# A mixture-of-experts layer with two streams of tokens: where the context's column-tiled down products stand in an expert's order of work

## The chip, the cores and the metric

The kernel runs on one core of one Trainium2 chip. The metric is the time of one execution on the device in microseconds; below it is the median of three executions. TensorE (PE) multiplies, VectorE (DVE) and ScalarE (ACT) work elementwise, GpSimd (POOL) here issues gathers and scatters, and SyncE (SP) issues the large loads.

## The reference

Two transformer layers are computed on 1024 latent tokens and 256 context tokens of width 1024. Each layer has attention of two kinds and a convolution, and then a mixture of 16 experts in which each expert picks its own tokens. Only the first layer sends the context through its experts too. What matters here is this part:

```python
def ec_moe(h, w_router, w_gate, w_up, w_down):
    bsz, n_tok, d = h.shape
    cap = EC_CAPACITY * n_tok // N_EXPERTS
    aff = jax.nn.softmax(jnp.einsum('bnd,de->bne', h, w_router).astype(jnp.float32), axis=-1)
    g, idx = lax.top_k(jnp.swapaxes(aff, 1, 2), cap)
    xs = jax.vmap(lambda hb, ib: hb[ib])(h, idx)
    hid = jax.nn.silu(jnp.einsum('becd,edf->becf', xs, w_gate)) * jnp.einsum('becd,edf->becf', xs, w_up)
    ye = jnp.einsum('becf,efd->becd', hid, w_down) * g[..., None].astype(h.dtype)
    return jax.vmap(lambda yb, ib: jnp.zeros((n_tok, d), h.dtype).at[ib.reshape(-1)].add(yb.reshape(-1, d)))(ye, idx)
```

An expert takes 128 latent tokens and 32 context tokens. Everything is float32.

## The kernel before, in words

**Steps and chunks.** The experts of the first layer run in `moe` (from line 2072) as 16 x 12 steps, numbered `i`; step `c` of expert `e` works on one chunk of that expert's weights, 128 x 2048 values, 1 MB. Chunks 0 to 7 are gate and up weights (a gate step: `mm_gu0`, lines 2145 and 2146), chunks 8 to 11 are down weights (a down step).

**Precision.** A chunk is split into a high part (`w_hi`, a copy on ACT to the faster 32-bit matmul type, line 2065) and a low part, the rest (`w_lo`, a subtraction on DVE, line 2071). The latent rows' down product `mm_d0` (lines 2226 to 2228) has for each of 4 pieces of a chunk three matmuls of 128 x 512: high hidden values with the high part, low hidden values with the high part, high hidden values with the low part. So the first two of each three read `hi` alone, and the third reads `lo`.

**The context's down product.** For 32 tokens a full product would fill a quarter of the array. `mm_dc` (line 2217) therefore puts four products side by side, each 32 columns wide, and sums their parts later (`ev_dc`). It reads the raw chunk, without any split, in full float32, which takes two passes a matmul: 8 passes a chunk in the trace. In the loop it stands ahead of `mm_d0` in each of the four down steps. For the last expert the down steps are written out behind the loop, and there the four chunks' `mm_dc` stand in a row ahead of all of `mm_d0`.

**Order.** The order on every engine is the order in which the program issues the instructions. A step issues its matmuls; then the evacuations of the step before (`ev_gu`, `ev_d`, `ev_dc`); then the high part of the chunk three steps ahead and the low part of the chunk two steps ahead (`self.w_hi(i + m - 1)`, `self.w_lo(l, i + m - 2, nc.vector)`, with four pairs of slots, m = 4); then the loads; then transposes of the next expert's gathered tokens (`xprep`, at c = 7 the latent rows, at c = 9 the context rows, line 2129). Besides, every seventh step loads 1 MB of the next layer's modulation weights (`adw`), and DVE reduces it in pairs of operations (`adj`, line 366) four and five steps later.

**Loads.** Raw chunks go round seven buffers (four `raw`, three `more`). All of them, and `adw`, are issued by SP in order; a load waits on SP until the buffer's last reader is done. The chunk in buffer `k` is followed there by chunk k + 7. A gate chunk's last reader is the subtraction `w_lo`, a down chunk's is `mm_dc`. The loop issues the load that follows gate chunk `k` two steps ahead of step `k`, the one that follows down chunk `k` at step `k`.

**PSUM.** Four tiles of two banks each ("gu") go round for gate products, transposes, the latent rows' down product `y` and the context's `yc`.

Of the kernel before, what the change touches and what calls it, by code (L numbers as in the profile page):

```python
# [209 lines left out]
class Kern:  # L210
# [18 lines left out]
    def rot(self, pool, shape, dt, name, n):  # L229
        i = self.cnt[name] = self.cnt.get(name, -1) + 1  # L230
        return self.one(pool, shape, dt, f"{name}{i % n}")
# [1843 lines left out]
    def moe(self, l, out):  # L2075
        nc, d = self.nc, self.d
        last = l == L - 1
# [22 lines left out]
        def gather(e):  # L2100
            x = p.tile([128, D], F32, name="xg", bufs=1)
            nc.gpsimd.indirect_dma_start(out=x, out_offset=None, in_=self.s_h2,
                                         in_offset=bass.IndirectOffsetOnAxis(ap=idx[:, e:e + 1], axis=0))
            xc = None
            if not last:
                xc = p.tile([32, D], F32, name="xgc", bufs=1)
                nc.gpsimd.indirect_dma_start(out=xc, out_offset=None, in_=self.s_h2c,
                                             in_offset=bass.IndirectOffsetOnAxis(ap=idxc[:32, e:e + 1], axis=0))
            S["x", e] = (x, xc)

        def xprep(e, h):
            x, xc = S["x", e]
            if h == 0:
                S["xt", e] = p.tile([128, KC, 2, nt], F32R, name="xt", bufs=1)
                w, cs, src = 128, slice(lat0, nt), x
            else:
                w, cs, src = 32, slice(0, 32), xc
            xt = S["xt", e]
            if last:
                for k in (0, 4):  # L2120
                    t = rot(ps, [128, 4, 128], F32, "gu", 8)
                    for j in range(4):
                        nc.tensor.transpose(t[:, j], src[:, (k + j) * 128:(k + j + 1) * 128], self.ident)  # L2123
                    nc.scalar.activation(xt[:, k:k + 4, 0], t, AF.Copy)
                    nc.vector.tensor_tensor(xt[:, k:k + 4, 1], t, xt[:, k:k + 4, 0].bitcast(F32), op=ALU.subtract)
                return
            t = rot(ps, [128, KC, 128], F32, "gu", 4)
            for j in range(KC):
                nc.tensor.transpose(t[:, j, :w], src[:, j * 128:(j + 1) * 128], self.ident[:w, :w])
            nc.scalar.activation(xt[:, :, 0, cs], t[:, :, :w], AF.Copy)  # L2130
            nc.vector.tensor_tensor(xt[:, :, 1, cs], t[:, :, :w], xt[:, :, 0, cs].bitcast(F32), op=ALU.subtract)  # L2131
# [79 lines left out]
        def mm_dc(e, c):  # L2211
            raw = S["raw", e * 12 + c].rearrange("p (k f) -> p k f", k=4)
            if c == 8:
                S["yc", e] = rot(ps, [128, 2, 512], F32, "gu", 4)
            yc, hc = S["yc", e][:, 0], S["hid", e][1]
            for k in range(4):
                nc.tensor.matmul(yc[32 * k:32 * k + 32], hc[:, (c - 8) * 2 + k // 2], raw[:, k], start=c == 8, stop=c == 11)

        def mm_d0(e, c, ns=(0, 1)):
            hi, lo = S["w", e, c]  # L2220
            hd = S["hid", e][0]
            y = S["y", e]
            for k in range(2):
                kk = (c - 8) * 2 + k
                for n in ns:
                    nc.tensor.matmul(y[:, n], hd[:, kk, 0], hi[:, k * 2 + n], start=kk == 0, stop=False)
                    nc.tensor.matmul(y[:, n], hd[:, kk, 1], hi[:, k * 2 + n], start=False, stop=False)  # L2227
                    nc.tensor.matmul(y[:, n], hd[:, kk, 0], lo[:, k * 2 + n], start=False, stop=kk == 7)

        def mm_d1(e, c):  # L2230
            hi, lo = S["w", e, c]
            hd = S["hid", e]
            n, kh = divmod(c - 8, 2)
            if kh == 0:
                S["y", e, n] = rot(ps, [128, 512], F32, "gu", 8)
            y = S["y", e, n]
            for k in range(4):
                kk = kh * 4 + k
                nc.tensor.matmul(y, hd[:, kk, 0], hi[:, k], start=kk == 0, stop=False)  # L2239
                nc.tensor.matmul(y, hd[:, kk, 1], hi[:, k], start=False, stop=False)  # L2240
                nc.tensor.matmul(y, hd[:, kk, 0], lo[:, k], start=False, stop=kk == 7)  # L2241

        def ev_dc(e):
            yc = S.pop(("yc", e))[:, 0]
            yo = rot(p, [64, 512], F32, "yoc", 1)
            nc.scalar.activation(yo, yc[64:128], AF.Copy)
            nc.vector.tensor_tensor(yo, yc[:64], yo, op=ALU.add)
            nc.vector.scalar_tensor_tensor(yo, yo, gc[:64, e:e + 1], self.g2[1], op0=ALU.mult, op1=ALU.mult)
            nc.gpsimd.indirect_dma_start(out=self.s_accc.rearrange("a (b c) -> (a b) c", b=2),
                                         out_offset=bass.IndirectOffsetOnAxis(ap=idx2[:, e:e + 1], axis=0),  # L2250
                                         in_=yo, in_offset=None, compute_op=ALU.add)

        def ev_d(e, n):
            ns = slice(n * 512, n * 512 + 512)
            y = S["y", e, n] if last else S["y", e][:, n]
            if n == 0:
                S["yo", e] = rot(p, [128, D], F32, "yo", 1)
            yo = S["yo", e]
            nc.vector.scalar_tensor_tensor(yo[:, ns], y, g[:, e:e + 1], self.g2[0][:, ns], op0=ALU.mult, op1=ALU.mult)  # L2259
            if n == 1:  # L2260
                nc.gpsimd.indirect_dma_start(out=self.s_acc[l],  # L2261
                                             out_offset=bass.IndirectOffsetOnAxis(ap=idx[:, e:e + 1], axis=0),
                                             in_=yo, in_offset=None, compute_op=ALU.add)
# [33 lines left out]
        n = len(steps)  # L2297
        np_ = 1 if last else 2
        xs = [9] if last else [7, 9]
        m = len(self.wslots)  # L2300
        nl = m + len(self.ring)
# [3 lines left out]
        for i in range(n - 2 if last else n - 4):  # L2305
            e, c = steps[i] if i < n else (None, None)
            pe, pc = steps[i - 1] if i > 0 else (None, None)
            if c == 2 and e + 1 < NE:
                gather(e + 1)
            if i < n:  # L2310
                if c < 8:
                    mm_gu(e, c)
                elif last:
                    mm_d1(e, c)
                else:
                    if c == 8:
                        S["y", e] = rot(ps, [128, 2, 512], F32, "gu", 4)
                    mm_dc(e, c)
                    mm_d0(e, c)
            if pc is not None:  # L2320
                if pc < 8:
                    ev_gu(pe, pc, 0)
                    if pc == 7 and not last:
                        ev_gu(pe, pc, 1)
                        ev_gu(pe, pc, 2)
                elif last:
                    if pc % 2:
                        ev_d(pe, pc // 2 - 4)
                elif pc == 11:
                    for h in range(2):  # L2330
                        ev_d(pe, h)
                    ev_dc(pe)
            if pc is not None and pc < 7 and not last:
                ev_gu(pe, pc, 1)
            if m <= i + m - 1 < n:
                self.w_hi(i + m - 1)
            if m <= i + m - 2 < n:
                self.w_lo(l, i + m - 2, nc.vector)
            while nl < n and nl - len(self.ring) <= (i if not last and (nl - len(self.ring)) % 12 > 7 else i + m - 2):
                self.w_load(l, nl)  # L2340
                nl += 1
            if pc is not None and last and pc < 8:
                ev_gu(pe, pc, 1)
            if last and i > n - 12:
                spare(i - n + 11)
            if pc is not None and pc < 7:
                ev_gu(pe, pc, 2)
            if i < n and c in xs and e + 1 < NE:
                xprep(e + 1, xs.index(c))
            if ad and i % 7 == 1:  # L2350
                adw = p.tile([128, 2, D], F32, name="adw")
                self.adaln_load(adw, l + 1, ad[0])
                todo = self.adaln_items(l + 1, ad.pop(0))
            elif todo and i % 7 in (5, 6):
                for f in todo[:2]:
                    f(adw, p.tile([128, D], BF16, name="adj"))
                todo = todo[2:]
        if last:
            self.close_last(l, out, E, g, mm_d1, lambda: rot(p, [128, D], F32, "yo", 1), S, p, ps)
        else:  # L2360

            e = NE - 1
# [162 lines left out]
```

## Time and profile before

| | |
|---|---|
| median of three executions | 2929.53 us (2923.95 to 2930.57) |
| the profiled execution's own time | 2927.74 us |
| its span, first to last instruction | 2926.0 us |
| PE busy, whole span | 2619.4 us (90%) |
| DVE busy, whole span | 2184.7 us (75%) |
| ACT busy, whole span | 1587.8 us (54%) |
| DMA | 682.85 MB, mean 233 GB/s |

The span holds, in this order: modulation and the first layer's projections, attention and routing (up to some 814 us), the first layer's experts (some 814 to 1625 us), the second layer's other parts, and the second layer's experts (from some 2290 us). A busy share is an average over all of these, and what the change is worth has to be read in the second. Times of instructions are microseconds from the start of the span. A matmul's listed duration includes its way through the array, so the pace of a stream is the distance between starts.

### The profile page before, as it was taken

The page shows a single profiled execution, that of the slowest core. Times are in us where ns is not written, and L with a number is a line of the kernel's source. Part 1 is how long each engine was busy: PE and PEld are TensorE (multiplying, and loading weights), DVE is VectorE, ACT ScalarE, POOL GpSimd, SP SyncE. Part 2 cuts the span into 40 slices and gives each one's busy share as a digit, 9 for nine tenths or more (in the row PEclk, how much of TensorE's full clock was granted, in tenths as well). Part 3 has the DMA queues.
Part 4 walks back from the last instruction along what each step waited for, and adds up shares of the span by engine and source line. Part 5 has one row for each costly group of instructions (what it writes and reads, how often), then busy time and mean ns, then how long its engine had stood idle before and what let it go on. Part 6 is the DMA issues. An engine that isn't in the chain of part 4 may idle for free. (4 is left out here: it accounts for less than half of the span.)

```text
span 2926.0 us, 37297 instructions
## 1 busy us (share of the span) xinstructions
PE 2619.4 (90%) x13657; PEld 2057.6 (70%) x13657; DVE 2184.7 (75%) x3048; ACT 1587.8 (54%) x2023; POOL 884.3 (30%) x652
## 2 busy tenths in 40 slices
PE   7998888979489999999999499999996699999995
PEld 4986544558379898888889388755575477777774
DVE  6366498458879998888887844557577788888888
ACT  3224666622345666665666353587422477777774
POOL 3046687332312120201110415686042111111113
PEclk8999999989689999999999699999997799999997
DMA  6254743493458897878886414474374699999983
GB/s 246 68 184 152 202 141 108 115 247 140 187 197 313 305 334 292 327 303 317 309 312 233 165 63 148 146 196 118 104 226 196 234 375 371 373 372 373 372 338 136
DMA packets 204352, 682.85 MB, mean 233 GB/s; under 512 B 25637, under 2 KB 97630, under 8 KB 148870
## 3 DMA queue, kind: packets, MB, share of 16 engines
q1 hardware_dynamic: 191834, 641.23, 60.6%
q0 software_dynamic: 12336, 39.25, 5.3%
q8 instruction: 107, 1.75, 0.3%
q14 instruction: 75, 0.61, 0.1%
HBM read 600.45 MB, written 79.84 MB: 233 GB/s over the span
## 5 line engine op out<-in xcount | busy, mean ns | idle before, releaser
L2071 DVE TENSOR_TENSOR lo<-raw,hi 128x2048 fp32r<-128x2048 f32 x284 | 641.0, 2284 | 6.4 <-ACT hi L2065 6.3
L2065 ACT ACTIVATE hi<-raw 128x2048 fp32r<-128x2048 f32 x289 | 551.8, 1912 | 83.5 <-PE gu L2185 36.9
L2145 PE MATMUL gu<-xt,hi 128*128 128x320 f32 x2048 | 528.7, 333 | 0.9 <-DVE xt L2131 0.9
L2146 PE MATMUL gu<-xt,lo 128*128 128x192 f32 x2048 | 513.6, 251 | 0.0
L1257 POOL TENSOR_TENSOR cy<-cy,csq 128x512 f32<-128x512 f32 (+1 forms) x300 | 386.2, 1302 | 110.5 <-ACT csq L1253 100.7
L2261 POOL DMA_INDIRECT s_acc<-yo,i x31 | 76.3, 2462 | 1120.3 <-DVE yo L2259 1120.3
L2146 PEld LDWEIGHTS gu<-xt,lo 128*128 128x128 f32 x2048 | 393.2, 192 | 0.6
L2145 PEld LDWEIGHTS gu<-xt,hi 128*128 128x128 f32 x2048 | 386.0, 188 | 1.8 <-DVE xt L2131 1.1
L1183 PE MATMUL O<-P,v 128*65 128x512 f32 (+7 forms) x592 | 280.7, 563 | 13.1 <-ACT P L1176 12.8
L1253 ACT ACTIVATE csq<-ch,cw 128x512 f32<-128x512 f32 (+1 forms) x300 | 199.4, 674 | 48.7 <-POOL cy L1257 44.7
L2184 PE MATMUL gu<-hi,xt 128*128 128x512 f32 x512 | 204.2, 399 | 0.0
L2185 PE MATMUL gu<-hi,xt 128*128 128x512 f32 x512 | 202.8, 396 | 0.0
L2186 PE MATMUL gu<-lo,xt 128*128 128x512 f32 x512 | 202.6, 396 | 0.0
L735 PE MATMUL pj<-hhi,whi 128*128 128x512 f32 (+1 forms) x512 | 188.7, 369 | 8.7 <-ACT whi L249 8.7
L737 PE MATMUL pj<-hhi,wlo 128*128 128x512 f32 (+1 forms) x512 | 188.1, 367 | 1.1 <-DVE wlo L252 1.1
L736 PE MATMUL pj<-hlo,whi 128*128 128x512 f32 (+1 forms) x512 | 188.1, 367 | 0.0
L2071 DVE TENSOR_TENSOR lo<-more,hi 128x2048 fp32r<-128x2048 f32 x80 | 182.1, 2284 | 0.0
L2065 ACT ACTIVATE hi<-more 128x2048 fp32r<-128x2048 f32 x80 | 152.1, 1906 | 19.5 <-PE gu L2227 11.4
L366 DVE CUSTOM_DVE_ANT_0 adj<-adw,srow,bmod 128x1024 bf16<-128x1024 f32 x96 | 133.9, 1395 | 33.2 <-DMA adw<-in_wmt 31.5
L1737 PE MATMUL po<-hi,ohi 128*128 128x512 f32 x288 | 121.7, 423 | 21.4 <-DVE ohi L1715 18.9
L1176 ACT ACTIVATE P<-ST 128x512 f32<-128x512 f32 (+1 forms) x200 | 114.3, 580 | 47.9 <-PE ST L1159 25.2
L2153 ACT ACTIVATE t<-gu 128x320 f32<-128x320 f32 x128 | 55.5, 433 | 119.3 <-PE gu L2146 119.1
(319 smaller groups left out, 5834.3 us busy)
## 6 DMA issues: line engine op xcount, KB each, us to landing
raw<-in_wmoe SPq DMA_DIRECT2D x289, 1024.0 KB
more<-in_wmoe SPq DMA_DIRECT2D x80, 1024.0 KB
adw<-in_wmt SPq DMA_DIRECT2D x24, 1024.0 KB
srow<-in_wmoe SPq DMA_DIRECT2D x15, 1024.0 KB
wraw<-in_win SPq DMA_DIRECT2D x26, 512.0 KB
x<-in_x SPq DMA_DIRECT2D x16, 512.0 KB
adw<-in_wmt SPq DMA_DIRECT2D x16, 512.0 KB
q<-s_q SPq DMA_DIRECT2D x64, 128.0 KB
```

The lines of the kernel that those rows point to most:

```text
L735: nc.tensor.matmul(o[:, :w], whi[:, k], hhi[:, k, sl], start=k == 0, stop=False)
L736: nc.tensor.matmul(o[:, :w], whi[:, k], hlo[:, k, sl], start=False, stop=False)
L1183: nc.tensor.matmul(o[:V1, o0:o0 + w], self.v[:, t["kt"], t["v"] * V1:t["v"] * V1 + V1], t["P"][:, :w], start=t["first"], stop=t["last"] is ...
L1253: nc.scalar.activation(z[:, :w], h, AF.Copy, scale=c)
L1257: nc.gpsimd.tensor_tensor(st["y"], st["y"], st.pop(("z", t))[:, :w], op=ALU.add)
L2065: self.nc.scalar.activation(h, self.S["raw", i], AF.Copy)
L2071: eng.tensor_tensor(lo, r, h.bitcast(F32), op=ALU.subtract)
L2145: nc.tensor.matmul(o[:, f, :320], hi[:, k, fs], xt[:, k], start=k == 0, stop=False)
L2146: nc.tensor.matmul(o[:, f, :192], lo[:, k, fs], xt[:, k, :192], start=False, stop=k == 7)
L2184: nc.tensor.matmul(o, xt[:, kk, 0], hi[:, k], start=kk == 0, stop=False)
L2185: nc.tensor.matmul(o, xt[:, kk, 1], hi[:, k], start=False, stop=False)
L2186: nc.tensor.matmul(o, xt[:, kk, 0], lo[:, k], start=False, stop=kk == 7)
```

## The change

In the first layer's loop the latent rows' `mm_d0` comes first in every down step. The context's `mm_dc` of all four chunks is issued at the last down step (c = 11), one behind the other, after `mm_d0`. So that the raw chunks are still there, the rule for loads changes: no load that would overwrite a down chunk of an expert is issued before step 11 of that expert. The last expert's own code is as it was, and so is the second layer.

```diff
@@ -2315,8 +2315,10 @@
                 else:
                     if c == 8:
                         S["y", e] = rot(ps, [128, 2, 512], F32, "gu", 4)
-                    mm_dc(e, c)
                     mm_d0(e, c)
+                    if c == 11:
+                        for k in range(8, 12):
+                            mm_dc(e, k)
             if pc is not None:
                 if pc < 8:
                     ev_gu(pe, pc, 0)
@@ -2336,7 +2338,10 @@
                 self.w_hi(i + m - 1)
             if m <= i + m - 2 < n:
                 self.w_lo(l, i + m - 2, nc.vector)
-            while nl < n and nl - len(self.ring) <= (i if not last and (nl - len(self.ring)) % 12 > 7 else i + m - 2):
+            while nl < n:
+                k = nl - len(self.ring)
+                if k > i + m - 2 or not last and k % 12 > 7 and i < k // 12 * 12 + 11:
+                    break
                 self.w_load(l, nl)
                 nl += 1
             if pc is not None and last and pc < 8:
```

## Rows read from the trace of the kernel before

**Rows 1.** Table by stretches: busy time by engine, granted clock, DMA share, GB/s.

```profile
870.00:1600.00 730.00, 730.00 (x5127) 638.14 (x5124) 627.85 (x677) 440.56 (x452) 118.53 (x58) 1.00 0.84 309
```

**Rows 2.** Timeline of PE, experts 1 and 7: start, length, line, tile, count.

```profile
906.75 1.06 PE L2217 MATMUL gu<-raw,hic 128*32 128x512 f32 x8
...
1208.31 1.07 PE L2217 MATMUL gu<-more,hic 128*32 128x512 f32 x8
1209.31 0.50 PE L2226 MATMUL gu<-hi,hid 128*128 128x512 f32 x1
1209.64 0.39 PE L2227 MATMUL gu<-hi,hid 128*128 128x512 f32 x1
...
1211.97 0.39 PE L2228 MATMUL gu<-lo,hid 128*128 128x512 f32 x1
1212.29 1.06 PE L2217 MATMUL gu<-more,hic 128*32 128x512 f32 x8
...
1216.28 0.68 PE L2129 MATMUL gu<-ident,xgc 32*128 32x32 f32 x8
1216.89 1.07 PE L2217 MATMUL gu<-more,hic 128*32 128x512 f32 x8
...
1224.77 0.31 PE L2145 MATMUL gu<-xt,hi 128*128 128x320 f32 x1
```

**Rows 3.** Timeline of PE, the last expert.

```profile
1609.51 1.92 PE L2217 MATMUL gu<-raw,hic 128*32 128x512 f32 x16
1611.25 1.90 PE L2217 MATMUL gu<-more,hic 128*32 128x512 f32 x16
1613.08 0.50 PE L2226 MATMUL gu<-hi,hid 128*128 128x512 f32 x1
```

**Rows 4.** Timeline of DVE, expert 7: low parts of chunks 10 and 11.

```profile
1212.52 2.29 DVE L2071 TENSOR_TENSOR lo<-more,hi 128x2048 fp32r<-128x2048 f32 x1
1214.72 2.29 DVE L2071 TENSOR_TENSOR lo<-raw,hi 128x2048 fp32r<-128x2048 f32 x1
```

**Rows 5.** Timeline of DVE, the same in experts 0, 1, 4, 5 and 8.

```profile
861.92 2.29 DVE L2071 TENSOR_TENSOR lo<-more,hi 128x2048 fp32r<-128x2048 f32 x1
...
913.49 2.29 DVE L2071 TENSOR_TENSOR lo<-more,hi 128x2048 fp32r<-128x2048 f32 x1
915.70 1.28 DVE L366 CUSTOM_DVE_ANT_0 adj<-adw,srow,bmod 128x1024 bf16<-128x1024 f32 x1
...
918.23 2.29 DVE L2071 TENSOR_TENSOR lo<-more,hi 128x2048 fp32r<-128x2048 f32 x1
...
1064.74 4.49 DVE L2071 TENSOR_TENSOR lo<-more,hi 128x2048 fp32r<-128x2048 f32 x2
...
1116.73 2.29 DVE L2071 TENSOR_TENSOR lo<-more,hi 128x2048 fp32r<-128x2048 f32 x1
...
1265.31 4.49 DVE L2071 TENSOR_TENSOR lo<-more,hi 128x2048 fp32r<-128x2048 f32 x2
```

**Rows 6.** Timeline of PE around two pauses, and stretches with their granted clock.

```profile
1997.77 0.27 PE L950 MATMUL S<-ident,m 128*8 128x128 f32 x1 [2.23 <-DVE m L1028]
1999.30:2002.60 3.30, 3.30 (x9) 1.96 (x8) 1.87 (x5) 3.20 (x7) 3.30 (x4) 0.50 0.11 25
...
1863.80 0.27 PE L950 MATMUL S<-ident,m 128*8 128x128 f32 x1 [1.82 <-DVE m L1028]
1862.00:1880.00 18.00, 14.67 (x79) 12.48 (x80) 11.61 (x26) 7.97 (x13) 5.13 (x4) 1.00 0.20 75
```

**Rows 7.** Timelines of SP, ACT and DVE as expert 8 starts; the page's GB/s.

```profile
1222.00 8.34 SPq L2060 DMA_DIRECT2D raw<-in_wmoe  x4
1224.74 1.92 ACT L2065 ACTIVATE hi<-more 128x2048 fp32r<-128x2048 f32 x1 [1.40 <-PE gu L2227]
1232.80 2.29 DVE L2071 TENSOR_TENSOR lo<-more,hi 128x2048 fp32r<-128x2048 f32 x1
GB/s 246 68 184 152 202 141 108 115 247 140 187 197 313 305 334 292 327 303 317 309 312 233 165 63 148 146 196 118 104 226 196 234 375 371 373 372 373 372 338 136
```

## The prediction

> **What bounds the kernel now.** I read the page first: slices 12 to 21 of its table of 40 are the first layer's experts, and PE shows 9 in all of them. The table by stretches then settles the stage: of the 730 us from 870 to 1600 PE is busy all 730.00, at a granted clock of 1.00 (the 2.4 GHz level), while DVE has 627.85 and ACT 440.56 [rows 1]. No wait of PE is left there, so each microsecond of PE work taken out is one microsecond gained, until another engine ends last, and the next is DVE at 86%. Hence the order of reading: PE's instructions around one expert's down steps for what the edit saves, then DVE's in the same places for what comes due earlier.
>
> **PE: what is removed.** In the timeline of expert 7 [rows 2] a group of four column-tiled products (8 passes, "x8") starts at 1208.31 and the down product behind it at 1209.31: 1.00 us. The first down matmul is then followed after 0.33 us, the others every 0.233 (1209.64 to 1211.97 is ten of them): 0.10 more behind each group. Ahead of a group that follows a down product there are 0.32 us (1211.97 to 1212.29) for 0.23: 0.09. The groups of chunks 8 and 10 follow transposes and have no such lead. Four groups cost 4 x 1.00 + 4 x 0.10 + 2 x 0.09 = 4.58 us. The four in one row stand in the trace already: the last expert, written out by hand, runs them from 1609.51 to 1613.08, 3.57 us for 32 passes [rows 3]. With one lead and one tail that is 3.76 us, a gain of 0.82.
>
> Against it: expert e+1's small transposes (1216.28 to 1216.89) now stand ahead of a down product and no longer of a column-tiled one. The trace before has no such junction; the nearest rows bound it by 0 (transposes to group: 0.61 us for the eight, with no lead to be seen) and 0.23 (a lone group's 1.00 less the 0.87 that one takes inside the row, 1609.51 to 1611.25 for two, and the tail of 0.10). I take 0.05, nearer to the transposes' own row. The exit from the row into the next expert's gate product I take as that into a down product. Per expert 0.77 us; experts 0 to 14 run the edited loop, the last is unchanged: 15 x 0.77 = 11.5 us. Bounds: 8.9 (0.23 at the junction) and 13.8 (nothing there, no tail into the gate product).
>
> The Trainium skill ("TensorEngine Tiling (Array Packing)", section Tiling Modes, Key Properties) says that a change of tiling mode, not just of tile, drains the array. The rows agree with a drain at each lone group. By this rule the small transposes, which use a quarter of the rows, would pay one on leaving as well, which is the junction's upper bound: by it the gain is 8.9 us, not 11.5.
>
> **What comes due earlier.** Counted from S, the start of chunk 8's group before, which is where the first down product starts after (S = 1208.31 for expert 7 and 50.26 us apart: 906.75 for expert 1 is six of these earlier). After: chunks 8 and 9 take 12 x 0.233 = 2.80 us each, the transposes 0.09 + 0.61, so chunk 10 starts at S + 6.3, and the first matmul that reads its low half is the third of the block, 0.5 later: S + 6.8. Chunk 11's is one block later: S + 9.6. Before, these were S + 10.1 (chunk 10 starts 1.00 after 1216.89) and S + 14.1. The groups were cover for DVE: chunk 10's low half is made behind the next expert's transposed input, the gate evacuations and whatever reductions of the next layer's modulation weights (the adj pairs, 2.5 us) are due, and DVE starts this at S whatever PE does later.
>
> Ends of DVE's low halves against S: expert 7 is the usual case: 1212.52 + 2.29 is S + 6.50 and 1214.72 + 2.29 is S + 8.70 [rows 4]: 0.3 and 0.9 us early, no stall; eight more experts lie within 0.7 of it. Where an adj pair stands ahead [rows 5]:
> - expert 0: 864.21, S + 7.72: PE waits 0.9 at chunk 10 (backlog from the stage's start);
> - expert 1: pairs ahead of both chunks: 915.78, S + 9.03: 2.2; then 920.52, S + 13.77, against 9.6 + 2.2: 2.0 more;
> - expert 4: the first of two in 4.49 us ends at 1067.0, S + 9.5: 2.7; chunk 11 then is in time;
> - expert 8: the same pattern, 1267.6, S + 9.0: 2.2;
> - expert 5: chunk 11 at 1119.02, S + 11.23: 1.6; expert 12 repeats it: 1.6.
> Together 13.2 us of PE waiting where before there was none. As DVE's own queue is not moved, no later step wins this back; once PE is the one that waits, its time is lost. Bounds: 10.5 (each of the seven waits 0.4 shorter) and 16 (0.4 longer: semaphores, and the 0.4 of the nearest of the eight).
>
> **Clock.** A PE pause of 2.23 us at 1995.5 (the wait noted at 1997.77) is followed by the 1.2 GHz level: 0.50 in 1999.30 to 2002.60; one of 1.82 us, up to 1863.80, is not: 1.00 in 1862 to 1880 [rows 6]. Half the clock for 3.3 us costs some 1.6 us. Three waits reach that size (experts 1, 4, 8). In expert 1 the slower PE only uses up the second wait; so 2 x 1.5 = 3.0 us, between 0 and 7 x 1.6 = 11.
>
> **Loads, SP and the rest.** Raw buffers of chunks 8 to 10 are kept to the end of the row. Before, SP issued their refills one by one; four go out in 8.34 us from 1222.00 [rows 7]. After, six are released within some 3.5 us of the row, the first about 2.5 us ahead of the next expert (G = 1224.77 in expert 7's case). At the 373 GB/s that the second layer's slices of the page sustain [rows 7], one load is 2.8 us; six end by about G + 17 with nothing else moving. The first is needed at ACT for the copy noted at 1224.74 (G, 1.92 us) and by DVE at 1232.80, G + 8.0. Landing at about G + 2.5 delays ACT's copy by 2.5 us, which ends at G + 4.4, 3.6 us before DVE takes it. A gate step is about 4.2 us ((50.26 - 16.46) / 8, with S to G 16.46), so the later loads gain some 1.4 us each on their use. Cost 0. Queued behind these on SP are the modulation weights of the next layer; where their issue falls into the last down step (experts 5 and 12), theirs is the seventh load, which ends at about G + 20, and DVE comes to them four gate steps on, at about G + 16. Most of these 4 us goes into the lead that DVE has on PE in gate steps; I take 0.2 each, 0.4 in all, bounds 0 and 8. If that lead went, each late load would cost its lateness in every expert. POOL's scatter of the latent rows is issued earlier, since that product now ends ahead of the row; nobody waits for it. The changed order of PSUM tiles costs nothing: the four buffers go round, and what the context's product takes over was emptied under the down products.
>
> **The sum.** -11.5 + 13.2 + 3.0 + 0.4 = +5.1 us on the profiled execution's own 2927.74 (span 2926.0): 2932.8. The median before is 1.8 above that execution, so the forecast in medians is 2934.5, 0.17% over 2929.53. What a measurement here can tell from no change is 0.2%, 5.9 us.
>
> **Rivals.**
> - DVE is no later than PE. For: in expert 1 chunk 11's low half ended 0.2 us after its block began and PE did not wait, so PE waits only where it reads. Against: the ends in rows 5 pass that point too. Then 11.5 us stand: 2918.0. Faster. If only half of the waits come, 2924.6 without a clock fall.
> - The clock falls after more of the waits than two. For: the engine was at the 2.4 GHz level for the whole stage because it never paused, and the pause of 2.23 us was enough. Against: 1.82 us was not. With all seven, 2927.74 - 11.5 + 13.2 + 11 + 1.8 = 2942. Slower by over 0.2% from the third fall on.
> - The burst of six comes too late. Place: ACT's copy for the next expert's chunk 3, then DVE. Price: it decides from 3.6 us of lateness past G + 2.5; 1 us beyond it in 15 experts is 15 more, 2949. Against: 3.6 us is more than one load takes.
> - The row does not pay (the junction and both ends cost all that is saved): 4 us worse than the forecast, 2938.
>
> **How the numbers follow.** Forecast 0.50; clock 0.22; burst or row 0.13; DVE in time 0.15. Forecast and its neighbours spread some 4 us each way, so a part of it passes +5.9. Faster 0.13, same 0.49, slower 0.38. The range reaches down to half of the waits and up to the clock's case: 2922 to 2943.
>
> **What would show it.** Right: in the stretch 870 to 1600 PE is no longer full; it waits some 13 us for DVE's low half, in experts 0, 1, 4, 5, 8 and 12 at the first matmul that reads it; expert 7's 16.46 us from S to G (1224.77) are about 15.7; the row takes 3.6 us; the clock is below 1.00 in short stretches behind experts 4 and 8. Wrong: no DVE wait (then the gain is visible), waits on ACT's copies or loads in gate steps, or a row of four that takes over 4 us.

## The result and the profile after

The changed kernel takes 2977.48 us (median of 4, 2973.78 to 2979.37) against 2926.81 us in the same session: a ratio of 1.016, 95% interval 1.0141 to 1.018. It is slower by some 47 us by the ratio, and by 50.7 between the two medians, where +5 was forecast and 2943 was the end of the range. The profiled execution has a span of 2977.3 us. Counted from the first gate product of the stage to the end of its last latent down product, the first layer's experts take 851.7 us (815.3 to 1667.0) and took 804.1 (820.4 to 1624.5): +47.6, so nearly all of it lies in this stage. What the span gains besides lies within what the parts ahead of the stage (814 to 824 us) and behind it (1298 to 1310 us) differ by from run to run.

The stretch table (same columns as [rows 1]) shows a PE that is no longer full:

```profile
870.00:1650.00 780.00, 743.02 (x5155) 659.11 (x5154) 630.59 (x680) 441.79 (x456) 119.81 (x57) 0.97 0.76 291
```

37 of the 780 us are pauses, and the granted clock has fallen to 0.97 on the mean. DVE has the same work as before: over the whole stage, 677.87 us from 815 to 1667, and 677.45 before from 820 to 1625. Who waited for whom in the stage, from the tables of waits of PE, DVE and SP (us in total, times, longest):

```profile
PE gu L2228 <- DVE lo L2071: 21.4, 12, 5.3
PE gu L2146 <- DVE lo L2071: 16.1, 4, 5.4
...
DVE adj L366 <- DMA adw<-in_wmt: 40.0, 7, 8.7
...
SPq L360 <- DMA adw<-in_wmt: 38.7, 5, 9.2
SPq L360 <- DVE modc L366: 20.0, 4, 10.8
```

The first row is the forecast's kind of wait, in down steps, though larger. The second is in gate steps, where none was forecast. The third row has no counterpart before: DVE stands 40 us for the next layer's modulation weights. SP's rows say that the next weights wait for their buffer in turn, so SP stands too.

Where nothing disturbs an expert, the saving is there. Expert 9 in the timeline of PE, to be laid beside [rows 2]:

```profile
1335.94 1.04 PE L2129 MATMUL gu<-ident,xg 128*128 128x128 f32 x8
1336.73 0.48 PE L2226 MATMUL gu<-hi,hid 128*128 128x512 f32 x1
1337.05 0.39 PE L2227 MATMUL gu<-hi,hid 128*128 128x512 f32 x1
...
1342.51 0.68 PE L2129 MATMUL gu<-ident,xgc 32*128 32x32 f32 x8
1343.12 0.50 PE L2226 MATMUL gu<-hi,hid 128*128 128x512 f32 x1
1343.92 0.40 PE L2226 MATMUL gu<-hi,hid 128*128 128x512 f32 x1
...
1348.91 3.64 PE L2217 MATMUL gu<-raw,hic 128*32 128x512 f32 x32
1352.48 0.42 PE L2145 MATMUL gu<-xt,hi 128*128 128x320 f32 x1
```

The row of four takes 3.57 us, to the hundredth what the last expert showed [rows 3]. The next gate product starts 15.75 us after the first down product (before, 16.46 us after the context group that stood there), and from gate product to gate product this expert takes 49.48 us against 50.26.

One of the gate pauses, from SP to PE (timelines of SP, ACT, DVE and PE, two stretches with their granted clock, DMA share and GB/s, and the DMA queues from 1133.75 to 1160.75):

```profile
1133.75 2.04 SPq L2060 DMA_DIRECT2D raw<-in_wmoe  x3
1136.28 1.29 SPq L2060 DMA_DIRECT2D more<-in_wmoe  x3
1137.63 0.45 SPq L360 DMA_DIRECT2D adw<-in_wmt  x1
...
1150.67 1.92 ACT L2065 ACTIVATE hi<-more 128x2048 fp32r<-128x2048 f32 x1
...
1149.95 2.28 DVE L2071 TENSOR_TENSOR lo<-raw,hi 128x2048 fp32r<-128x2048 f32 x1
1160.75 1.29 DVE L366 CUSTOM_DVE_ANT_0 adj<-adw,srow,bmod 128x1024 bf16<-128x1024 f32 x1 [8.52 <-DMA adw<-in_wmt]
...
1164.29 2.29 DVE L2071 TENSOR_TENSOR lo<-more,hi 128x2048 fp32r<-128x2048 f32 x1
...
1136.15 0.41 PE L2145 MATMUL gu<-xt,hi 128*128 128x320 f32 x1
...
1166.63 0.53 PE L2146 MATMUL gu<-xt,lo 128*128 128x192 f32 x1 [5.43 <-DVE lo L2071]
...
1156.00:1161.00 5.00, 5.00 (x41) 4.97 (x39) 0.25 (x1) 1.36 (x1) 0.00 (x0) 1.00 1.02 421
1164.40:1171.00 6.60, 4.37 (x18) 4.37 (x19) 6.11 (x8) 4.39 (x6) 0.00 (x0) 0.50 1.02 426
...
q1 hardware_dynamic: 1109, 8.17, 78.3%
q0 software_dynamic: 416, 1.31, 18.7%
```

SP issues the weights at 1137.63 behind six raw loads; they land 23.1 us later. DVE is done with chunk 5's low part at 1152.2 and then stands, in order, at the reduction, though chunk 6, whose high part ACT has ready at 1152.6, holds the next low part that PE needs. Chunk 6's low part starts at 1164.29 and PE pauses 5.43 us. The DMA engines are full meanwhile (1.02, 421 GB/s): the transfers that used to trickle through the down steps all come at once. From 1164.40 to 1171.00, the last part of the pause and the work behind it, TensorE's granted clock is at its 1.2 GHz level (0.50); before the pause the engine had been busy without a gap.

### The profile page after: what moved, and what is told of

The parts are those of the page before. It is cut to its first block, busy times and chain, and to the rows that moved or that the text cites. A ratio compares the mean times of both kernels' runs of the same rounds, so it can differ in the third digit from the quotient of the medians.

```text
span 2977.3 us, 37303 instructions
## 1 busy us (share of the span) xinstructions
PE 2632.3 (88%) x13657; PEld 2077.1 (70%) x13657; DVE 2187.4 (73%) x3048; ACT 1586.1 (53%) x2023; POOL 888.6 (30%) x652
## 5 line engine op out<-in xcount | busy, mean ns | idle before, releaser
L2145 PE MATMUL gu<-xt,hi 128*128 128x320 f32 x2048 | 537.1, 336 | 1.1 <-DVE xt L2131 0.9
L2146 PE MATMUL gu<-xt,lo 128*128 128x192 f32 x2048 | 517.1, 252 | 16.1 <-DVE lo L2071 16.1
L2261 POOL DMA_INDIRECT s_acc<-yo,i x31 | 76.3, 2462 | 1152.2 <-DVE yo L2259 1152.2
L2228 PE MATMUL gu<-lo,hid 128*128 128x512 f32 x256 | 107.1, 418 | 21.5 <-DVE lo L2071 21.4
```

The lines of the kernel that those rows point to most:

```text
L2145: nc.tensor.matmul(o[:, f, :320], hi[:, k, fs], xt[:, k], start=k == 0, stop=False)
L2146: nc.tensor.matmul(o[:, f, :192], lo[:, k, fs], xt[:, k, :192], start=False, stop=k == 7)
```

## The experiments

Each was timed beside the kernel before on the same chip (its medians there: 2926.81 us for the changed kernel, 2926.51 for the loads' rule alone, weights loaded once, weights issued by POOL and no weights, 2927.84 for the last row, 2928.3 for the others), and the ratios are to these. "Stage" is the first layer's experts, measured as above, in the profiled execution.

| kernel | median us | ratio to before, interval | stage us | PE pauses us | DVE waits for weights us |
|---|---|---|---|---|---|
| before | 2926.81 | | 804.1 | 0 | 0 |
| changed | 2977.48 | 1.016 (1.0141 to 1.018) | 851.7 | 37.7 | 40.0 |
| loads' rule alone | 2925.71 | 1.0 (0.9978 to 1.0022) | 804.9 | 0 | 0 |
| changed, weights loaded once | 2934.21 | 1.0021 (1.0003 to 1.0039) | 810.8 | 11.2 | 0 |
| changed, weights issued by POOL | 2940.0 | 1.0049 (1.003 to 1.0068) | 817.5 | 15.3 | 2.7 |
| changed, no weights | 2910.79 | 0.9956 (0.9941 to 0.997) | 792.2 | 0 | 0 |
| buffers held alone | 2989.78 | 1.0196 (1.0179 to 1.0213) | 865.7 | 41.5 | 37.4 |
| changed, weights placed anew | 2940.16 | 1.0036 (1.0022 to 1.005) | 816.2 | 14.6 | 0 |
| before, weights placed anew | 2926.33 | 0.9993 (0.9982 to 1.0005) | 804.3 | 0 | 0 |
| changed, weights early, two buffers | 2912.76 | 0.9953 (0.994 to 0.9967) | 792.7 | 0 | 0 |

**The loads' rule alone.** The diff's second half in the kernel before; `mm_dc` stays ahead of each `mm_d0`.

> The kernel before with the changed rule for loads alone: the context's products stay ahead of each latent product, the refills of a down chunk's buffer wait for step 11. Theory A (the next layer's modulation weights land behind the burst of six on SP's queue, DVE stands in order before their reduction, its low parts come late): DVE still waits some 40 us in 7 places for them; PE has more cover in the down steps than in the changed kernel, so only the pauses in gate steps (experts 3, 6, 10, 13: 24 us with the slow clock) and a part of those in experts 4, 7, 11 stay: 2945 to 2962 us. Theory B (the price is the lost cover in the down steps): no pause, 2927 us, as before. Theory C (ACT's copies late by the burst): above 2945 with PE pauses that no DVE wait for the modulation weights precedes.

Nothing changed: PE is busy for all of the stage, the time is theory B's, and theory A's range is missed. The expectation of theory A was wrong in one point. The rule moves the place of a load in SP's order, not the moment its buffer comes free; that is set by the last reader, and `mm_dc` still read chunk 8 in step 8. SP still issues the refills of expert 7's down chunks one by one over 8.91 us, where the changed kernel issues six within 4 us (1133.75 to 1137.57 above):

```profile
1207.88 8.91 SPq L2060 DMA_DIRECT2D more<-in_wmoe  x3
```

So the issue order by itself costs nothing, and the run does not test a late release; it can't decide between A and B.

**Buffers held alone.** The missing test: the order on PE as before, the new rule, and a late reader.

```diff
+            if not last and c == 11:
+                for k in range(8, 11):
+                    nc.vector.tensor_copy(keep[:, k - 8:k - 7], S["raw", e * 12 + k][:, :1])
```

> The kernel before in its order on PE, with the changed rule for loads, and the raw chunks 8 to 10 really held: DVE copies one column of each in the last down step, so that their buffers come free some 14 us after the first down product, as in the changed kernel. Theory A (late release alone makes the modulation weights late, through SP's queue): DVE waits for them 25 to 45 us in all, PE pauses in gate steps of four experts, and, with more cover in the down steps, less there than in the changed kernel: 2938 to 2960 us. Theory D (the held buffers only hurt together with the shorter down steps): no wait of DVE for DMA above 5 us, 2925 to 2930 us.

2989.78 us, worse than the changed kernel, though PE has all its cover in the down steps. The tables of waits of DVE and PE:

```profile
DVE adj L366 <- DMA adw<-in_wmt: 37.4, 7, 8.2
...
PE gu L2146 <- DVE lo L2071: 32.8, 8, 7.6
PE gu L2217 <- DVE sg L2154: 7.6, 3, 4.4
PE gu L2228 <- DVE lo L2071: 1.1, 1, 1.1
```

The same seven places wait for the weights, and PE pays in gate steps. Holding three buffers some steps longer is enough for the loss, theory A; theory D falls. The time lies beyond the 2960 expected. The stage is 61.6 us longer than before: 41.5 are pauses, and undisturbed experts take 50.69 us here, not 50.26, some 6 us if it is so in all 15. Why they do, and what the rest is, I did not trace. Against the changed kernel the gain on PE (11.9 us, below) is missing too.

**Weights loaded once.** The changed kernel with all reductions in their places, but on the first load's data.

```diff
-                adw = p.tile([128, 2, D], F32, name="adw")
-                self.adaln_load(adw, l + 1, ad[0])
+                if i == 1:
+                    adw = p.tile([128, 2, D], F32, name="adw")
+                    self.adaln_load(adw, l + 1, ad[0])
```

> The changed kernel with the modulation weights loaded only once in the stage: all their reductions stay on DVE in their places but read the first load's data, so the next layer's modulation is not the reference's, and the other loads are left out. Theory A: no DVE wait for DMA. Left are 0.78 us gained in each of 15 experts (11.7) and the waits for lost cover in experts 0, 1, 4, 5, 8 and 12, 13 us by the prediction and some 18 with the slow clock: 2928 to 2935 us. Theory B: nothing changes, 2977 us. Theory C: 2965 us or more, as the burst is still there.

No wait for DMA is left on DVE. What is left are the prediction's waits for lost cover and one short wait in expert 3 (table of waits, and four of the timeline of PE, in experts 1, 3, 4 and 8):

```profile
PE gu L2228 <- DVE lo L2071: 11.2, 7, 2.6
...
920.06 0.50 PE L2228 MATMUL gu<-lo,hid 128*128 128x512 f32 x1 [2.14 <-DVE lo L2071]
1021.82 0.50 PE L2228 MATMUL gu<-lo,hid 128*128 128x512 f32 x1 [0.34 <-DVE lo L2071]
1074.17 0.50 PE L2228 MATMUL gu<-lo,hid 128*128 128x512 f32 x1 [2.61 <-DVE lo L2071]
1277.84 0.50 PE L2228 MATMUL gu<-lo,hid 128*128 128x512 f32 x1 [2.13 <-DVE lo L2071]
```

The stage is 40.8 us shorter than the changed kernel's. So 40.8 us of the change's cost hang on the weights' loads, and +6.7 is what the rest of the change does to the stage, near the +5.1 forecast for the whole.

**Weights issued by POOL.**

```diff
-                self.adaln_load(adw, l + 1, ad[0])
+                nc.gpsimd.dma_start(adw, d["wmt"][((l + 1) * 48 + ad[0] - 12) // 2])
```

> The changed kernel with the modulation weights issued by POOL in place of SP, at the same place in the program; the same bytes at about the same time, but no longer behind the burst in one queue. Theory A in its form of queue order: the weights land within 10 us or so, DVE's waits for them shrink from 40 us to under 10, 2928 to 2942 us. Theory A in its form of bandwidth (the burst takes all of the engines): waits stay above 20 us, 2950 us or more. Theory B: 2977 us.

The same bytes at the same place in the program, and 34 us of the stage come back; DVE waits 2.7 us once. Two things changed with the queue: the weights share the DMA engines with the burst and don't queue behind it, and POOL, which has no raw loads to issue, often issues them earlier. The Trainium skill ("DMA: Bandwidth & Descriptors", section Queues, rings and completion order) has each DMA engine take one queue's descriptors in order and alternate between queues; the trace agrees as far as it goes. Of the seven loads that DVE waited for in the changed kernel, five are issued during or behind the burst here too; they land 12.6 to 17.2 us after their issue, where DVE had the same five 17.4 to 21.2 us after it from SP's queue. The other two go out ahead of the burst and land after 5.1 us. The times to landing of one of each (issued at 988.60 and 1131.53):

```profile
DMA to landing us min/median/max: 12.6/12.6/12.6
...
DMA to landing us min/median/max: 5.1/5.1/5.1
```

So both take part; how much of the 34 us each is worth, the run doesn't tell.

**No weights.** Neither loads nor reductions; a constant stands in for the next layer's modulation.

```diff
-        ad, todo = list(range(0, 48, 2)) if not last else [], []
+        ad, todo = [], []
+        if not last:
+            nc.vector.memset(self.modc[1], 0.5)
```

> The changed kernel without loads and reductions of the next layer's modulation weights in this stage (a constant stands in for that modulation). Theories A and B together (every pause comes from these reductions, either late or in the way): only expert 0's pause of 0.8 us or less is left, PE's gain of 0.78 us in 15 experts stands alone: 2915 to 2918 us. Theory C: PE still pauses in gate steps, above 2940 us.

Stage 792.2 us, 11.9 less than before: the change's gain by itself, with the burst of raw loads still there and no pause. So theory C, raw loads that come too late for ACT, makes no pause here. DVE has less to do in this run without the reductions; the last run, with all of them, has the burst and no pause too, and so theory C has no part in the loss. ACT does wait for raw data in the changed kernel, in 35 places of up to 2.4 us, but DVE takes the copies later.

**Weights placed anew.** In 15 experts a load at gate step 6, reduced at down step 10; in 9 a second one ahead of the burst at step 11, reduced at gate steps 1 and 4.

```diff
-            if ad and i % 7 == 1:
...
+            if not last and c == 11 and nb < 9:
+                adw, todo = fetch(ad[0])
...
+            if not last and c == 6 and e < NE - 1 or not last and c in (1, 4, 10):
```

> The changed kernel with the modulation weights placed anew: one load at gate step 6, reduced at down step 10, in 15 experts; one at step 11 ahead of the burst on SP, reduced at gate steps 1 and 4 of the next expert, in 9. No reduction stands between the next expert's transposes and the low parts of chunks 10 and 11, and no load of weights stands behind the burst. Theory A and B: DVE waits for no DMA, PE pauses less than 2 us in all, 0.78 us are gained in 15 experts: 2914 to 2918 us. If the reductions hurt at any place (DVE simply lacks the time): 2920 us or more with pauses elsewhere.

Missed. DVE no longer waits for weights, but experts 1 to 8 still pause, 15 times in all, of up to 1.5 us (waits of PE in the stage; then of ACT from 960 to 1280 and from 1290 to 1560):

```profile
PE gu L2228 <- DVE lo L2071: 8.8, 8, 1.1
PE gu L2146 <- DVE lo L2071: 5.8, 7, 1.5
...
ACT hi L2065 <- DMA raw<-in_wmoe: 34.4, 17, 5.6
...
ACT hi L2065 <- DMA raw<-in_wmoe: 9.0, 6, 4.2
```

Where the second load goes ahead of the burst, ACT waits up to 5.6 us for raw chunks. SP stands there too: from 960 to 1280 it waits 48.8 us in six places for a reduction to free the one buffer of the weights, with the burst behind that load. How much of ACT's wait comes from this and how much from the load itself I did not trace. From expert 9 on, with one load an expert, there is no pause, at 49.5 us an expert. Load time or DVE time could both be the cause, and the next run tells them apart.

**Before, weights placed anew**, the control.

> The kernel before with the same new places of the modulation weights, as a control: PE was full there, so no change is expected from any theory, 2925 to 2929 us, with PE busy in all of the stage. A gain here would say that the new places help by themselves.

As expected: no difference, PE full.

**Weights early, two buffers.** Both loads of an expert go out while SP has no raw load to issue.

```diff
-            if ad and i % 7 == 1:
-                adw = p.tile([128, 2, D], F32, name="adw")
-                self.adaln_load(adw, l + 1, ad[0])
-                todo = self.adaln_items(l + 1, ad.pop(0))
-            elif todo and i % 7 in (5, 6):
-                for f in todo[:2]:
-                    f(adw, p.tile([128, D], BF16, name="adj"))
+            if ad and e < NE - 1 and (c == 6 or c == 8 and e < 9):
+                t = ad.pop(0 if c == 8 else max(0, 8 - e))
+                adw = p.tile([128, 2, D], F32, name="adw", bufs=2)
+                self.adaln_load(adw, l + 1, t)
+                todo += [(f, adw) for f in self.adaln_items(l + 1, t)]
+            elif todo and c in (1, 4, 10):
+                for f, w in todo[:2]:
+                    f(w, p.tile([128, D], BF16, name="adj"))
                 todo = todo[2:]
```

> The changed kernel with two buffers for the modulation weights; both loads of an expert are issued on SP where it has no raw load to issue (behind gate step 6, and in 9 experts behind down step 8), so that they land ahead of the burst; reduced at down step 10, gate steps 1 and 4. Theory A: in the placement tried before, the weights ahead of the burst made the raw chunks late (ACT waited up to 5.6 us for them); with that gone, pauses fall from 14.4 us to under 3 and the gain of 0.78 us in 15 experts is left: 2915 to 2920 us. If DVE has too little time in the experts with six reductions, whatever the loads do, pauses of 1 to 2 us stay in experts 0 to 8: 2930 to 2940 us.

2912.76 us, a ratio of 0.9953 (0.994 to 0.9967), faster than both kernels, and below the expected range. The stretch table, and SP in expert 8's down steps:

```profile
870.00:1560.00 690.00, 690.00 (x4908) 616.26 (x4900) 604.99 (x656) 425.34 (x434) 109.16 (x56) 1.00 0.83 316
...
1244.07 0.91 SPq L360 DMA_DIRECT2D adw<-in_wmt  x2
1264.46 1.62 SPq L2060 DMA_DIRECT2D raw<-in_wmoe  x2
1266.24 1.68 SPq L2060 DMA_DIRECT2D more<-in_wmoe  x3
```

PE is full again at 1.00, with all reductions done and the burst as large as in the changed kernel. The two weights' loads are out 20 us ahead of it. The experts with six reductions take 49.5 us like the others, so DVE had the time; the pauses of the placement before came from the loads. The place of the loads and the second buffer were changed together, so the run does not say whether the earlier place alone would do. The stage is 792.7 us, the gain of the kernel without weights but for 0.5.

## Why the prediction was wrong

- **The gain on PE** was forecast at 11.5 us and is 11.9 (no weights) or 11.4 (early, two buffers). Per expert 0.78 for 0.77. Two errors of it nearly cancel: the small transposes ahead of a down product cost 0.10 (1343.12 to 1343.92 is 0.80 for three matmuls at 0.70), not 0.05, and not the 0.23 of the upper bound; and the latent transposes hand over to a down product after 0.79 us, not the 0.96 they had ahead of a column-tiled group (below, and 1208.31 in [rows 2]), of which the first down matmul gives 0.09 back (1336.73 to 1337.05 is 0.32 for 0.23).

```profile
1207.35 1.03 PE L2129 MATMUL gu<-ident,xg 128*128 128x128 f32 x8
```

- **The lost cover**, 13.2 us of PE waits: right. With the loads out of the way PE pauses at six of the seven forecast matmuls, 0.84, 2.14, 2.61, 1.54, 2.13 and 1.56 us for 0.9, 2.2, 2.7, 1.6, 2.2 and 1.6. The seventh, expert 1's second (2.0), does not wait at all: the slow clock used it up, as forecast. One wait of 0.34 us, in expert 3, was not in the list.
- **The clock**, 3.0 us: right in that run, with slow stretches behind the waits of experts 1, 4 and 8 and no others. This is luck in part: the limit between 1.82 and 2.23 us that it rests on does not hold in other runs (last section). Gain, cover and clock then leave +6.7 us of the stage, where these three terms came to +4.7. Most of the 2 us between lies in the restarts: expert 5, with one pause of 1.54 us and no slow clock, takes 51.29 us and not 49.48, so a pause costs some 0.27 us more than its listed length, 1.9 us over seven.
- **The step that failed** is in "Loads, SP and the rest": "Most of these 4 us goes into the lead that DVE has on PE in gate steps; I take 0.2 each, 0.4 in all, bounds 0 and 8." It measures 40.8 us (changed kernel less weights loaded once). Three things in it were wrong. First, the count: only the weights issued in the last down step were taken (experts 5 and 12). Those issued in the next expert's first three steps stand behind the same burst; seven reductions wait, not two. Second, the time: in the case shown above (G = 1136.15) DVE came to the reduction at G + 16.1, as forecast, but the seventh load had landed at G + 24.6 and not at G + 20. A load was priced at 2.8 us with nothing else moving; in the 27 us to the landing, SP's queue moved 8.17 MB, where seven loads are 7.34, and gathers and scatters took 18.7% of the DMA engines' time. Third, the lead: DVE's 8.5 us of waiting cost PE 5.4 us at once, so DVE's lead was 3 us, and slow clock came on top. The changed kernel has nine slow stretches for the three of the run with weights loaded once, and PE pauses of 37.7 us for 11.2.
- The rival "the burst comes too late" looked at the right queue and named the wrong transfer: ACT's raw chunks kept their margin, as worked out. The clock rival happened as a consequence, not as a cause.

## What to carry to other kernels

When buffers are held longer, the refills don't only come later: they come together, and everything else on that queue stands behind them. List each transfer that shares the queue, with the instruction that waits for it and what is queued behind that instruction on its in-order engine; here a reduction that nobody needed before the next layer held up the one subtraction that PE needed next. Transfers that are not urgent belong in the gap that the holding leaves, ahead of the burst, with a buffer of their own.

## What was not expected of the hardware

A short PE pause can already be followed by the lower level of TensorE's clock, and the length of the pause does not decide it. In the changed kernel, pauses and the stretches behind them (timeline, and stretches with their granted clock):

```profile
1002.95 0.36 PE L2146 MATMUL gu<-xt,lo 128*128 128x192 f32 x1 [1.92 <-DVE lo L2071]
1003.90:1007.20 3.30, 3.30 (x16) 3.30 (x15) 3.23 (x8) 1.97 (x3) 0.00 (x0) 0.50 1.01 427
...
1130.05 0.50 PE L2228 MATMUL gu<-lo,hid 128*128 128x512 f32 x1 [1.55 <-DVE lo L2071]
1131.00:1140.00 9.00, 9.00 (x70) 5.76 (x69) 8.10 (x7) 1.99 (x2) 2.95 (x2) 1.00 0.57 213
```

After 1.55 us the clock stayed at 1.00, after 1.92 it was 0.50; in [rows 6] a pause of 1.82 us had left it at 1.00. No limit comes out of this. With the weights placed anew, pauses of 1.1 us were followed by either level, and with the weights issued by POOL one of 2.13 us, at the place in expert 8 where the run with weights loaded once fell to 0.50, left it at 1.00:

```profile
960.79 0.50 PE L2228 MATMUL gu<-lo,hid 128*128 128x512 f32 x1 [1.11 <-DVE lo L2071]
961.60:964.90 3.30, 3.30 (x9) 2.58 (x8) 3.30 (x3) 2.57 (x4) 0.00 (x0) 0.50 0.02 5
...
1013.53 0.50 PE L2228 MATMUL gu<-lo,hid 128*128 128x512 f32 x1 [1.12 <-DVE lo L2071]
1014.00:1020.00 6.00, 6.00 (x34) 4.06 (x36) 5.96 (x6) 4.31 (x4) 0.00 (x0) 1.00 0.01 3
...
1281.55 0.50 PE L2228 MATMUL gu<-lo,hid 128*128 128x512 f32 x1 [2.13 <-DVE lo L2071]
1282.00:1292.00 10.00, 10.00 (x66) 6.15 (x65) 8.51 (x8) 4.90 (x5) 1.64 (x1) 1.00 0.32 99
```

With the buffers held alone even a pause of 2.81 us, up to 948.93, was followed by 1.00. What decides it besides stays open here; a price for the clock fall has to carry both cases.
